# Attention transposes with a longer lag and a fourth buffer, and ScalarE as issuer of result stores, folds and four weight loads

## The chip, the cores and the metric

The kernel runs on one core of a Trainium2 chip. The metric is device microseconds of one execution, and less is better. The core has five instruction streams that matter here: TensorE (PE, with its weight loads shown as PEld), VectorE (DVE), ScalarE (ACT), GpSimd (POOL) and SyncE (SP). Each runs its own instructions in order and waits on semaphores for the others. A DMA transfer is started by an instruction on one of these engines, and the transfer itself runs on 16 DMA engines that all share.

## The reference

One layer of a hybrid decoder for a prompt of 2048 tokens and for 64 sample tokens (8 requests of 8 tokens) with a key/value cache of 2048 rows each. Cut to what matters:

```python
h = rms_norm(x, g_norm); proj = h @ w_in            # 1024 -> 3584
u, va, za, q, k, vb, zb = split(proj)               # q, k are RMS-normalised per head
a_out = rms_norm(u * (tril(w_s) @ rms_norm(va) + b_s)) * silu(za)   # mixer A, chunks of 128
for (w, r) in ((128, 1), (512, 4), (2048, 16)):     # mixer B, 8 heads of 64
    # query t attends to t - j*r, j = 0..w//r: regrouped by residue class,
    # blocks of 128 queries against their own and the previous block of keys
    s = q @ k.T * SCALE (masked); m = max(s); p = exp(s - m); den = sum(p)
    o_r = p @ v / den;  lse_r = m + log(den)
b_out = sum_r softmax(lse)_r * o_r                  # combine the three patterns
b = rms_norm(b_out) * silu(zb)
h = x + concat(a_out, b) @ w_out
y = h + sigmoid(h @ w_ple_gate) * rms_norm(p @ w_ple)
```

The outputs are y for prompt and samples, the window buffers k and v, the new k and v rows of the samples and the normalised va rows. Inputs and outputs are float32.

## The kernel before

All matrices are split into a high and a low float16 half, and a product is made of three float16 matmuls (two for the samples). The program has three stages in time.

The **projection stage** (0 to about 900 us) makes eight chunks of columns of `w_in` in the order A0, B0, B1, A1, B2, B3, A2, A3. A B chunk holds q, k, v and gate of one pair of heads, an A chunk holds u, va and za of one group. For a chunk, `wprep` loads eight blocks of weights (L351) into `wst` and converts them. `gemm` (L465 to L478) then runs 24 matmuls for each of 16 blocks of 128 tokens (L473). The 64 sample rows stand below them: their two halves come out in the upper and lower half of the partitions, `fold` (L480) copies the lower half (L483), moves it up by a DMA (L484) and adds. `b_evac`, `b_norm`, `b_trans`, `a_evac` and so on take the results out of PSUM; the evacuation of the gates of an A chunk is L617.

**Attention** runs inside this stage. There are 160 units, each one half of a group of four blocks, for 4 head pairs, 3 patterns and 4 groups. A unit has three steps:

- first (L733): `scores` makes the score matmuls (L823), masks them and takes the maximum on DVE (L829, L834), the exponentials on ACT (L838), the high half of the probabilities into tile `pc` on ACT (L841) and the low half on DVE (L842);
- mid (L761): one DMA transpose of `pc` into tile `pT`, issued by SP (L763);
- second (L765): `stage_c`, the products of `pT` with the values on PE (L869 to L871). After each second unit ACT moves the sums out of PSUM into `rec` (L875), and a DMA stores them to DRAM (L883) in `r1d`, `r2d` or `r3d`, one for each pattern. There are 96 of these stores.

The order of this work is set by `Pump` (L69 to L145). It keeps a modelled time `now`, which every two gemm matmuls move forward by their modelled length (L478). A unit's transpose becomes due `P_LAG` after its scores (L110), its product `T_LAG` after the transpose, and no more than `depth` units stand in each of the two waiting lists (L93, L102). The order written in this way is then placed on each engine by the scheduler of the framework, which goes by its own model. Tiles rotate: a tag with n buffers lets n tiles be alive, and the instruction that wants the next one waits for the last reader of the oldest. `pc` has 3 buffers, as `pT`.

When all groups of a head pair are stored, `comb_load` (L886) loads the three results (`rl`, L891) and the stored gate (`gzl`, L894), `combine` (L897) mixes and normalises them on DVE and ACT, its last two steps being L925 and L926, and stores the result to `catd` (L928).

In the **output stage** (about 960 us to the end) `p3_load` loads a block of `catd` (L1031), `halves_T` splits it (L995) and transposes it on SP (L996) into `Tc`, and `gemm2` makes the output and gate products (L1008). The weights of this stage are converted by `wprep3` (L965). The sample attention (`sample`, L1200) runs beside it on all engines. Among its tiles are K3 and qB (L1260, L1263, L1264) and V tiles, which share the tags of `pT`, `pc` and others. Between 900 and 960 us lies the transition: the last combine, its store, load, split and transpose must be through before the first output matmul.

Every DMA counts on one of eight completion semaphores, taken in turn over the whole program. An instruction that issues a DMA therefore also waits until the DMA eight places earlier has landed, whoever issued that one.

Of the kernel before, what the change touches and what calls it, by code (L numbers as in the profile page):

```python
# [11 lines left out]
F16 = mybir.dt.float16  # L12
F32 = mybir.dt.float32
# [8 lines left out]
P = 128  # L22
# [3 lines left out]
TS = 64  # L26
# [18 lines left out]
W_V3 = 3000.0  # L45

QK_LAG = 9000.0
P_LAG = 8500.0
T_LAG = 6500.0

PAIR_NS = 33700.0
# [96 lines left out]
def tile_hymba_gmlp_dilated_attn_step(  # L148
# [6 lines left out]
    nc = tc.nc  # L155
# [21 lines left out]
    cst = ctx.enter_context(tc.tile_pool(name="cst", bufs=1))  # L177
    sml = ctx.enter_context(tc.tile_pool(name="sml", bufs=4))
    drm = ctx.enter_context(tc.tile_pool(name="drm", bufs=1, space=DRAM))
    pump = Pump(3, P_LAG, T_LAG)  # L180
    uid = [0]

    def nm(s):
        uid[0] += 1
        return f"{s}_{uid[0]}"
# [78 lines left out]
    wk = ctx.enter_context(tc.tile_pool(name="wk", bufs=2))  # L264
# [76 lines left out]
    def wprep(kind, i, fast=False, room=None):  # L341
# [3 lines left out]
        for kp in range(4):  # L345
            t = room[:, kp] if room is not None else q4t([P, 2, 512], F32, "wst")
            for k2 in range(2):
                r0 = (2 * kp + k2) * P
                src = win[r0:r0 + P, c0:c0 + 512 * ns].rearrange("p (s c) -> p s c", c=512)[:, :, P * i:P * i + P]
                with after(ahead[0]) if room is not None else nullcontext():  # L350
                    nc.sync.dma_start(t[:, k2, :ncol].rearrange("p (s c) -> p s c", c=P), src)  # L351
                if room is not None:
                    yield 0.0
            st.append(t)
# [125 lines left out]
    def fold(g, n, tag, bufs=2):  # L480

        c = wk.tile([P, 512], F32, name=nm("fold"), tag=tag, bufs=bufs)
        nc.scalar.activation(c[TS:, :n], g[TS:, :n], AF.Copy)  # L483
        nc.sync.dma_start(c[:TS, :n], c[TS:, :n])  # L484

        def end():
            nc.vector.tensor_tensor(c[:TS, :n], c[:TS, :n], g[:TS, :n], op=ALU.add)
            return c
        return end
# [4 lines left out]
    def b_group(hp, jg, njt, m):  # L494
        ss = small(16, "bss", 2)
        if m < P:
            t = wk.tile([P, 512], F32, name=nm("sb"), tag="sb", bufs=1)
            cut = lambda a, b: t[:, a:b].unsqueeze(1)
            return dict(raw=cut(0, 256), vo=cut(256, 384), gz=cut(384, 512), ss=ss, n=njt, m=m, jg=jg, hp=hp)
        pump.run(lambda: len(v_open) < 3)  # L500
        v_open.append(0)
        raw = wk.tile([P, 4, 256], F32, name=nm("raw"), tag="raw", bufs=2)
        v16 = wk.tile([P, 4, 258], F16, name=nm("v16"), tag="v16", bufs=3)
        vo = wk.tile([P, 4, P], F32, name=nm("vo"), tag="tmpA", bufs=2)
        gz = wk.tile([P, 4, P], F32, name=nm("gz"), tag="gz", bufs=2)
        vv = v16.rearrange("p j (h c) -> p j h c", h=2)
        nc.vector.memset(vv[:, :, :, 64:65], 1.0)
        return dict(raw=raw, ss=ss, v16=v16, vv=vv, vo=vo, gz=gz, n=njt, m=m, jg=jg, hp=hp)
# [91 lines left out]
    def a_group(g, jg, njt, m):  # L600
        ss = small(4, "ass", 2)
        if m == P:
            ua = wk.tile([P, 4, 256], F32, name=nm("ua"), tag="raw", bufs=2)
            gz = wk.tile([P, 4, P], F32, name=nm("agz"), tag="gz", bufs=2)
        else:
            t = wk.tile([P, 512], F32, name=nm("sb"), tag="sb", bufs=1)
            ua, gz = t[:, 0:256].unsqueeze(1), t[:, 256:384].unsqueeze(1)
        u, va = ua[:, :, 0:128], ua[:, :, 128:256]
        return dict(ua=ua, u=u, va=va, gz=gz, ss=ss, n=njt, m=m, jg=jg, g=g)
# [200 lines left out]
    def scores(QH, QL, keys, r, sub):  # L810
# [26 lines left out]
            for h in range(2):  # L837
                nc.scalar.activation(sm4[:, s, h], sm4[:, s, h], AF.Exp, bias=r[:, sl + s, h, HD + 1:HD + 2])  # L838
        n = ns * 2 * kw
        pc = wk.tile([P, 1024], F16, name=nm("pc"), tag="pc", bufs=3)  # L840
        nc.scalar.activation(pc[:, :n], smv, AF.Copy)  # L841
        nc.vector.tensor_tensor(pc[:, n:2 * n], smv, pc[:, :n], op=ALU.subtract)  # L842
        return pc, n, 4 * ns * (kw * 0.416 + 8)
# [3 lines left out]
    def stage_c(hp, pat, grp, sub, r, pT):  # L847
# [26 lines left out]
        if sl + ns == 2:  # L874
            nc.scalar.activation(r[:, :, :, 0:65], po[:, :, :, 0:65], AF.Copy)  # L875
            rc = r.rearrange("p j h c -> p j (h c)")
            if pat == 3:
                dst = r3d[hp].rearrange("(p g j) c -> g p j c", g=4, j=4)[grp]
            elif pat == 2:
                dst = r2d[hp][grp * 512:(grp + 1) * 512].rearrange("(p j) c -> p j c", j=4)  # L880
            else:
                dst = r1d[hp][grp * 512:(grp + 1) * 512].rearrange("(j p) c -> p j c", p=P)
            nc.sync.dma_start(dst[:, s0:s0 + 2], rc)  # L883
        return ns * 6 * nb * 36.0

    def comb_load(hp, jg):  # L886
# [313 lines left out]
    def sample(hp):  # L1200
# [14 lines left out]
        seq = quads[0] + quads[1]  # L1215

        def load(name, src, tag="v"):
            t = wk.tile([P, 4, P], F32, name=nm(name), tag=tag, bufs=3)
            nc.sync.dma_start(t, src)
            return t  # L1220
        Ks = [loadK(seq[0]), loadK(seq[1])]
# [14 lines left out]
        for n in range(NB + 1):  # L1236
# [19 lines left out]
            for th in range(2 if n < NB else 0):  # L1256
                ts_ = slice(th * 4, th * 4 + 4)
                K3 = wk.tile([96, 4, P], F32, name=nm("K3"), tag="pT", bufs=3)
                nc.sync.dma_start(K3, ck[b, 0:1536, cs].rearrange("(i t) d -> i t d", t=16)[:, ts_])
                qB = wk.tile([96, 4, P], F32, name=nm("qB"), tag="pc", bufs=3)  # L1260
                src = qd[b * 8 + th * 4:b * 8 + th * 4 + 4, cs]
                nc.sync.dma_start(qB, src.unsqueeze(0).to_broadcast([96, 4, P]))
                nc.gpsimd.tensor_tensor(K3, K3, qB, op=ALU.mult)  # L1263
# [45 lines left out]
                           for b, tag in zip(quads[n % 2], tags[(n + 2) % 3])]  # L1309

        def V3load(src, tag):
            t = wk.tile([96, 4, P], F32, name=nm("V3"), tag=tag, bufs=3)
            nc.sync.dma_start(t, src)
            return t
        V3s = []
# [283 lines left out]
```

## Time and profile before

| | |
|---|---|
| device time, 3 runs | 1482.63, 1478.48, 1474.4 us; median 1478.48 us |
| profiled execution | 1471.11 us |
| its span (first to last instruction) | 1469.4 us |
| mean granted TensorE clock | 0.954 of full speed |
| busy: PE, DVE, ACT, POOL | 1296.9, 999.6, 821.8, 315.7 us |
| DMA | 271.32 MB, 185 GB/s in the mean |

Busy time leaves out what an engine spends on issuing DMAs, so the lines of SP in the views, named SPq, are issue times: how long the instruction held the queue. Start times count from the first instruction. In a view of waits, a row says which engine stood idle in front of an instruction of which line, and what released it. Numbers like L883 are lines of the program before. The changed program has one line more from L352 on, so L883 is there L884.

### The profile page before, as it was taken

The page shows a single profiled execution, that of the slowest core. Times are in us where ns is not written, and L with a number is a line of the kernel's source. Part 1 is how long each engine was busy: PE and PEld are TensorE (multiplying, and loading weights), DVE is VectorE, ACT ScalarE, POOL GpSimd, SP SyncE. Part 2 cuts the span into 40 slices and gives each one's busy share as a digit, 9 for nine tenths or more (in the row PEclk, how much of TensorE's full clock was granted, in tenths as well). Part 3 has the DMA queues.
Part 4 walks back from the last instruction along what each step waited for, and adds up shares of the span by engine and source line. Part 5 has one row for each costly group of instructions (what it writes and reads, how often), then busy time and mean ns, then how long its engine had stood idle before and what let it go on. Part 6 is the DMA issues. An engine that isn't in the chain of part 4 may idle for free.

```text
span 1469.4 us, 26262 instructions
## 1 busy us (share of the span) xinstructions
PE 1296.9 (88%) x8600; PEld 674.0 (46%) x8600; DVE 999.6 (68%) x3018; ACT 821.8 (56%) x2269; POOL 315.7 (21%) x279
## 2 busy tenths in 40 slices
PE   4899998998898897899788985569998998999998
PEld 2564454544564554455455653224443443444343
DVE  4675776777777698777778788885455456456364
ACT  5785778966679677687677884553222122123122
POOL 8221001102101111100120025311152143134001
PEclk9899999999999999999999998779999999999999
DMA  5954598799847989978996798976899799989542
GB/s 145 235 132 114 124 173 182 173 222 226 193 112 165 206 188 209 178 185 189 222 213 145 154 247 216 288 173 170 203 210 245 181 203 229 230 184 231 137 88 65
DMA packets 589592, 271.32 MB, mean 185 GB/s; under 512 B 323184, under 2 KB 571056, under 8 KB 589456
## 3 DMA queue, kind: packets, MB, share of 16 engines
q1 hardware_dynamic: 587472, 268.00, 80.7%
q0 software_dynamic: 1984, 1.66, 0.7%
q8 instruction: 67, 1.10, 0.3%
q14 instruction: 69, 0.57, 0.1%
HBM read 136.94 MB, written 55.08 MB: 131 GB/s over the span
## 4 chain that ended last, share of the span: by engine, by line
PE 44%; DMA 23%; DVE 14%; ACT 11%; issue 4%; SPq 3%; POOL 1%; DVEq 0%; ACTq 0%; POOLq 0%
PE psg L473 14%; PE psg L1008 11%; PE pss L1008 10%; DMA pT<-pc 6%; DMA rl<-r2d 2%; DVE sm L829 2%; ACT sm L838 2%; DMA K<-in_cache_k_dram 2%; DMA qB<-qd 2%; DMA wst<-in_w_in_dram 2%; PE pso L1343 2%; DVE pc L842 2%; PE pso L1248 2%; ACT kc L715 1%; DMA rl<-r3d 1%
## 5 line engine op out<-in xcount | busy, mean ns | idle before, releaser
L473 PE MATMUL psg<-wt,xT 128*128 128x512 f16 (+1 forms) x3072 | 640.6, 363 | 31.3 <-DVE agz L617 26.5
L473 PEld LDWEIGHTS <-xT 128*128 128x128 f16 x3072 | 301.7, 100 | 299.7 <-issue 44.3
L193 POOL TENSOR_TENSOR sm<-sm,mhalf 128x1 f32<-128x1 f32 (+5 forms) x115 | 145.6, 1271 | 790.4 <-DVE sm L532 324.6
L838 ACT ACTIVATE sm<-sm,rec 128x256 f32<-128x256 f32 (+1 forms) x384 | 151.7, 459 | 38.9 <-DVE rec L834 35.8
L829 DVE CUSTOM_DVE_ANT_0 sm<-pss,mask,psc 128x256 f32<-128x256 f32 (+1 forms) x384 | 145.1, 419 | 12.2 <-PE pss L823 8.5
L1008 PEld LDWEIGHTS <-Tc 128*128 128x128 f16 x800 | 76.8, 99 | 116.0 <-issue 28.5
L1263 POOL TENSOR_TENSOR K<-K,qB 96x512 f32<-96x512 f32 x64 | 94.1, 1475 | 161.2 <-DMA qB<-qd 62.3
L842 DVE TENSOR_TENSOR pc<-sm,pc 128x512 f16<-128x512 f32 (+1 forms) x160 | 104.2, 653 | 34.1 <-ACT pc L841 32.7
L1008 PEld LDWEIGHTS <-Th 128*128 128x128 f16 x800 | 76.7, 98 | 109.0 <-issue 15.3
L995 ACT ACTIVATE hl<-x,sm 128x1024 f16<-128x1024 f32 (+1 forms) x17 | 19.5, 1148 | 147.3 <-DVE sm L976 132.4
L869 PEld LDWEIGHTS <-pT 128*128 128x128 f16 x600 | 57.1, 98 | 96.1 <-DMA pT<-pc 90.5
L1008 PE MATMUL psg<-w,Th 128*128 128x512 f16 x400 | 95.8, 381 | 5.0 <-DMA Th<-hl 5.0
L841 ACT ACTIVATE pc<-sm 128x512 f16<-128x512 f32 (+1 forms) x160 | 96.0, 603 | 7.2 <-DMA pT<-pc 6.2
L1008 PE MATMUL psg<-w,Tc 128*128 128x512 f16 x400 | 97.0, 386 | 2.8 <-DMA Tc<-hl 2.8
L1264 DVE TENSOR_REDUCE blk<-K 96x8 f32<-96x512 f32 x64 | 43.4, 680 | 79.5 <-POOL K L1263 79.5
L1008 PE MATMUL pss<-w,Tc 128*128 128x512 f16 x400 | 96.0, 382 | 0.0
L1008 PE MATMUL pss<-w,Th 128*128 128x512 f16 x400 | 93.4, 379 | 0.0
L823 PEld LDWEIGHTS <-qk 128*128 128x128 f16 x960 | 74.2, 120 | 29.3 <-issue 5.9
L1100 POOL TENSOR_TENSOR tg<-tg,x 128x1024 f32<-128x1024 f32 (+1 forms) x16 | 37.6, 2348 | 153.9 <-DVE tg L1099 141.8
L869 PE MATMUL pso<-v,pT 128*128 128x65 f16 x248 | 32.2, 201 | 42.4 <-DMA pT<-pc 42.4
L869 PE MATMUL pso<-vt,pT 128*128 128x65 f16 x352 | 43.5, 195 | 28.9 <-DMA pT<-pc 28.8
L715 ACT ACTIVATE kc<-qk 128x512 f16<-128x512 f16 x72 | 58.9, 872 | 13.8 <-DMA qk<-qkd 8.5
(321 smaller groups left out, 2239.5 us busy)
## 6 DMA issues: line engine op xcount, KB each, us to landing
qB<-qd SPq DMA_DIRECT2D x64, 192.0 KB
K<-in_cache_k_dram SPq DMA_DIRECT2D x64, 192.0 KB
V<-in_cache_v_dram SPq DMA_DIRECT2D x64, 192.0 KB
vt<-vscr SPq DMA_DIRECT2D x32, 258.0 KB
K<-in_cache_k_dram SPq DMA_DIRECT2D x32, 256.0 KB
cat<-catd SPq DMA_DIRECT2D x16, 512.0 KB
x<-in_x_prompt_dram SPq DMA_DIRECT2D x16, 512.0 KB
V<-in_cache_v_dram SPq DMA_DIRECT2D x32, 256.0 KB
```

The costliest lines, as they stand in the source:

```text
L193: nc.gpsimd.tensor_tensor(y, src, mhalf[:p, :n], op=ALU.pow)
L473: last_mm[0] = nc.tensor.matmul(g[:, :ncol], lhsT=l, rhs=r, start=(n == 0), stop=(n == (23 if j < NT else 15)))
L715: nc.scalar.activation(t[:, h], src[:, h], AF.Copy)
L823: nc.tensor.matmul(pss[:, s, h, b * w:(b + 1) * w], lhsT=Q[:, h, qs], rhs=keys(h, k), start=(i == 0 and b == 0), stop=(i == 1 and b == n - 1))
L829: nc.vector.tensor_tensor_reduce(sm4[:, s, h], pss[:, s, h], mk, psc, -3.0e38, op0=ALU.add, op1=ALU.max, accum_out=mx[:, i:i + 1])
L838: nc.scalar.activation(sm4[:, s, h], sm4[:, s, h], AF.Exp, bias=r[:, sl + s, h, HD + 1:HD + 2])
L841: nc.scalar.activation(pc[:, :n], smv, AF.Copy)
L842: nc.vector.tensor_tensor(pc[:, n:2 * n], smv, pc[:, :n], op=ALU.subtract)
L869: nc.tensor.matmul(po[:, q, h, 0:65], lhsT=H, rhs=v[:, vs_, a:a + 65], start=(bi == 0), stop=False)
L1008: last_mm[0] = nc.tensor.matmul(gs[hf], lhsT=o[part][:, kt], rhs=w[:, kt % 2, half, :], start=(n[hf] == 0), stop=(n[hf] == (3 if m == P el ...
L1263: nc.gpsimd.tensor_tensor(K3, K3, qB, op=ALU.mult)
L1264: nc.vector.tensor_reduce(s3[:, b, :, ts_].rearrange("p h t -> p t h"), K3.rearrange("p t (h d) -> p t h d", d=HD), axis=AX.X, op=ALU.add)
```

## The change

It has four parts. `P_LAG` grows from 8500 to 11500 modelled ns, `Pump` may hold four units in each list, and the tag `pc` has four buffers (also for the sample tiles that use this tag). To make room for the fourth, the tile `sb` of folded sample rows, which had a buffer of its own, now uses the single buffer of `gzl`, which `comb_load` uses too. The 96 result stores and the 14 moves of folded rows are issued by ScalarE's queue (`nc.scalar`) in place of SyncE's. Of the eight weight loads of the first chunk (the call of `wprep` with `fast`), the four with odd index are issued by ScalarE too.

```diff
--- before.py
+++ after.py
@@ -45,7 +45,7 @@
 W_V3 = 3000.0
 
 QK_LAG = 9000.0
-P_LAG = 8500.0
+P_LAG = 11500.0
 T_LAG = 6500.0
 
 PAIR_NS = 33700.0
@@ -177,7 +177,7 @@
     cst = ctx.enter_context(tc.tile_pool(name="cst", bufs=1))
     sml = ctx.enter_context(tc.tile_pool(name="sml", bufs=4))
     drm = ctx.enter_context(tc.tile_pool(name="drm", bufs=1, space=DRAM))
-    pump = Pump(3, P_LAG, T_LAG)
+    pump = Pump(4, P_LAG, T_LAG)
     uid = [0]
 
     def nm(s):
@@ -348,7 +348,8 @@
                 r0 = (2 * kp + k2) * P
                 src = win[r0:r0 + P, c0:c0 + 512 * ns].rearrange("p (s c) -> p s c", c=512)[:, :, P * i:P * i + P]
                 with after(ahead[0]) if room is not None else nullcontext():
-                    nc.sync.dma_start(t[:, k2, :ncol].rearrange("p (s c) -> p s c", c=P), src)
+                    (nc.scalar if fast and k2 else nc.sync).dma_start(
+                        t[:, k2, :ncol].rearrange("p (s c) -> p s c", c=P), src)
                 if room is not None:
                     yield 0.0
             st.append(t)
@@ -481,7 +482,7 @@
 
         c = wk.tile([P, 512], F32, name=nm("fold"), tag=tag, bufs=bufs)
         nc.scalar.activation(c[TS:, :n], g[TS:, :n], AF.Copy)
-        nc.sync.dma_start(c[:TS, :n], c[TS:, :n])
+        nc.scalar.dma_start(c[:TS, :n], c[TS:, :n])
 
         def end():
             nc.vector.tensor_tensor(c[:TS, :n], c[:TS, :n], g[:TS, :n], op=ALU.add)
@@ -494,7 +495,7 @@
     def b_group(hp, jg, njt, m):
         ss = small(16, "bss", 2)
         if m < P:
-            t = wk.tile([P, 512], F32, name=nm("sb"), tag="sb", bufs=1)
+            t = wk.tile([P, 512], F32, name=nm("sb"), tag="gzl", bufs=1)
             cut = lambda a, b: t[:, a:b].unsqueeze(1)
             return dict(raw=cut(0, 256), vo=cut(256, 384), gz=cut(384, 512), ss=ss, n=njt, m=m, jg=jg, hp=hp)
         pump.run(lambda: len(v_open) < 3)
@@ -603,7 +604,7 @@
             ua = wk.tile([P, 4, 256], F32, name=nm("ua"), tag="raw", bufs=2)
             gz = wk.tile([P, 4, P], F32, name=nm("agz"), tag="gz", bufs=2)
         else:
-            t = wk.tile([P, 512], F32, name=nm("sb"), tag="sb", bufs=1)
+            t = wk.tile([P, 512], F32, name=nm("sb"), tag="gzl", bufs=1)
             ua, gz = t[:, 0:256].unsqueeze(1), t[:, 256:384].unsqueeze(1)
         u, va = ua[:, :, 0:128], ua[:, :, 128:256]
         return dict(ua=ua, u=u, va=va, gz=gz, ss=ss, n=njt, m=m, jg=jg, g=g)
@@ -837,7 +838,7 @@
             for h in range(2):
                 nc.scalar.activation(sm4[:, s, h], sm4[:, s, h], AF.Exp, bias=r[:, sl + s, h, HD + 1:HD + 2])
         n = ns * 2 * kw
-        pc = wk.tile([P, 1024], F16, name=nm("pc"), tag="pc", bufs=3)
+        pc = wk.tile([P, 1024], F16, name=nm("pc"), tag="pc", bufs=4)
         nc.scalar.activation(pc[:, :n], smv, AF.Copy)
         nc.vector.tensor_tensor(pc[:, n:2 * n], smv, pc[:, :n], op=ALU.subtract)
         return pc, n, 4 * ns * (kw * 0.416 + 8)
@@ -880,7 +881,7 @@
                 dst = r2d[hp][grp * 512:(grp + 1) * 512].rearrange("(p j) c -> p j c", j=4)
             else:
                 dst = r1d[hp][grp * 512:(grp + 1) * 512].rearrange("(j p) c -> p j c", p=P)
-            nc.sync.dma_start(dst[:, s0:s0 + 2], rc)
+            nc.scalar.dma_start(dst[:, s0:s0 + 2], rc)
         return ns * 6 * nb * 36.0
 
     def comb_load(hp, jg):
@@ -1215,7 +1216,7 @@
         seq = quads[0] + quads[1]
 
         def load(name, src, tag="v"):
-            t = wk.tile([P, 4, P], F32, name=nm(name), tag=tag, bufs=3)
+            t = wk.tile([P, 4, P], F32, name=nm(name), tag=tag, bufs=4 if tag == "pc" else 3)
             nc.sync.dma_start(t, src)
             return t
         Ks = [loadK(seq[0]), loadK(seq[1])]
@@ -1257,7 +1258,7 @@
                 ts_ = slice(th * 4, th * 4 + 4)
                 K3 = wk.tile([96, 4, P], F32, name=nm("K3"), tag="pT", bufs=3)
                 nc.sync.dma_start(K3, ck[b, 0:1536, cs].rearrange("(i t) d -> i t d", t=16)[:, ts_])
-                qB = wk.tile([96, 4, P], F32, name=nm("qB"), tag="pc", bufs=3)
+                qB = wk.tile([96, 4, P], F32, name=nm("qB"), tag="pc", bufs=4)
                 src = qd[b * 8 + th * 4:b * 8 + th * 4 + 4, cs]
                 nc.sync.dma_start(qB, src.unsqueeze(0).to_broadcast([96, 4, P]))
                 nc.gpsimd.tensor_tensor(K3, K3, qB, op=ALU.mult)
@@ -1309,7 +1310,7 @@
                            for b, tag in zip(quads[n % 2], tags[(n + 2) % 3])]
 
         def V3load(src, tag):
-            t = wk.tile([96, 4, P], F32, name=nm("V3"), tag=tag, bufs=3)
+            t = wk.tile([96, 4, P], F32, name=nm("V3"), tag=tag, bufs=4 if tag == "pc" else 3)
             nc.sync.dma_start(t, src)
             return t
         V3s = []
```

Three places show how the instructions stand. The first is SP's queue in an early stretch of attention, at the first groups of pattern 1 (`r1d`). Before:

```order
L883 DMA r1d_107<-rec_1640 128x2x132
L558 DMA zscr_103<-gz_1580 128x4x128
L763 DMA_TRANSPOSE pT_1948<-pc_1783 128x8x128
L351 DMA wst_2982<-in_w_in_dram 128x3x128 x2
L763 DMA_TRANSPOSE pT_1966<-pc_1803 128x4x128
L555 DMA out_dram<-ko_1860 128x4x128
L593 DMA_TRANSPOSE qk_256_1551<-qkc_1869 128x6x128
L593 DMA_TRANSPOSE qk_256_1551<-qkc_1875 128x6x128
L883 DMA r1d_107<-rec_1674 128x2x132
L763 DMA_TRANSPOSE pT_1983<-pc_1820 128x4x128
```

After:

```order
L764 DMA_TRANSPOSE pT_1853<-pc_1702 128x8x128
L559 DMA zscr_103<-gz_1580 128x4x128
L351 DMA wst_3005<-in_w_in_dram 128x3x128 x2
L764 DMA_TRANSPOSE pT_2035<-pc_1813 128x4x128
L556 DMA out_dram<-ko_1893 128x4x128
L892 DMA rl_4280<-r1d_107 128x4x132
L764 DMA_TRANSPOSE pT_2037<-pc_1830 128x4x128
L594 DMA_TRANSPOSE qk_256_1551<-qkc_1902 128x6x128
```

The two `r1d` stores are gone from between the transposes; a load `rl` of a combine has moved up.

The second place is ACT's queue around the evacuation `rec_1674`, whose store is the second of the two above. Before:

```order
L367 ACTIVATE junk_3082,sm_3079<-wst_2982,gno 128x384
L875 ACTIVATE rec_1674<-pso_1931 128x4x65
L838 ACTIVATE sm_1952<-sm_1952,rec_1950 128x128 x2
L841 ACTIVATE pc_1820<-sm_1809 128x256
L523 ACTIVATE vo_1896<-psg_2010,sm_1256 128x128
L525 ACTIVATE th_2130<-psg_2010,sm_1256 128x128
L841 ACTIVATE pc_1963<-sm_1952 128x256
L584 ACTIVATE qkc_1881<-raw_1577 128x2x64
```

After:

```order
L839 ACTIVATE sm_1819<-sm_1819,rec_1800 128x128 x2
L876 ACTIVATE rec_1674<-pso_1976 128x4x65
L524 ACTIVATE vo_1929<-psg_1932,sm_1256 128x128
L526 ACTIVATE th_2017<-psg_1932,sm_1256 128x128
L842 ACTIVATE pc_1830<-sm_1819 128x256
L884 DMA r1d_107<-rec_1674 128x2x132
L586 ACTIVATE qkc_1902<-raw_1577 128x256
L586 ACTIVATE qkc_1908<-raw_1577 128x256
```

The store stands on ACT, four rows behind the evacuation that feeds it and ahead of the conversion of the keys (`qkc`).

The third place is DVE at the transition, where the last steps of a combine (`gzl<-rl,gzl`, followed by its store) stand between conversions of output weights (`w<-w3st`) and sums of sample products (`blk<-K`). Before:

```order
L1264 TENSOR_REDUCE blk<-K_2441_13639 96x4x2
L925 TENSOR_TENSOR rl_12553<-rl_12553,sm_12678 128x8x64
L965 SCALAR_TENSOR_TENSOR w_2246_12769<-w3st_12312,sm_12701,w_2246_12769 128x512
L1264 TENSOR_REDUCE blk<-K_2446_13662 96x4x2
L965 SCALAR_TENSOR_TENSOR w_2246_12769<-w3st_12312,sm_12701,w_2246_12769 128x512
L965 SCALAR_TENSOR_TENSOR w_2247_12774<-w3st_12344,sm_12701,w_2247_12774 128x512
L1264 TENSOR_REDUCE blk<-K_2448_13668 96x4x2
L965 SCALAR_TENSOR_TENSOR w_2247_12774<-w3st_12344,sm_12701,w_2247_12774 128x512
L926 TENSOR_TENSOR gzl_12559<-rl_12553,gzl_12559 128x512
L965 SCALAR_TENSOR_TENSOR w_2250_12809<-w3st_12346,sm_12701,w_2250_12809 128x512
```

After:

```order
L618 SCALAR_TENSOR_TENSOR agz_12835<-th_12998,psg_12919 128x128
L1188 TENSOR_SCALAR blk<-blk 128x64
L1192 CAST sc_12868<-blk 128x16
L902 TENSOR_TENSOR sm_12933<-rl_12787,rl_12789 128x8
L924 TENSOR_SCALAR sm_12781<-sm_12781,sm_7116 128x8
L1194 TENSOR_SCALAR blk<-sc_12868,blk 128x16
L926 TENSOR_TENSOR rl_12613<-rl_12613,sm_12781 128x8x64
L966 SCALAR_TENSOR_TENSOR w_2227_12642<-w3st_12208,sm_12640,w_2227_12642 128x512
L927 TENSOR_TENSOR gzl_12619<-rl_12613,gzl_12619 128x512
L966 SCALAR_TENSOR_TENSOR w_2227_12642<-w3st_12208,sm_12640,w_2227_12642 128x512
```

Before, four weight conversions and two sample sums stand between the last two steps of the combine, and after it one conversion.

## Rows read from the trace of the kernel before

**Rows 1.** page, part 1: busy time, share of the span, instructions

```profile
PE 1296.9 (88%) x8600; PEld 674.0 (46%) x8600; DVE 999.6 (68%) x3018; ACT 821.8 (56%) x2269; POOL 315.7 (21%) x279
```

**Rows 2.** windows: stretch, length, busy by engine, clock, DMA share, GB/s

```profile
150.00:900.00 750.00, 664.21 (x5366) 385.69 (x5364) 573.31 (x2067) 564.69 (x1634) 112.72 (x84) 0.96 0.85 186
900.00:960.00 60.00, 31.40 (x131) 14.42 (x132) 53.98 (x109) 26.04 (x86) 26.43 (x19) 0.74 1.04 260
960.00:1470.00 510.00, 477.41 (x2366) 203.60 (x2364) 282.80 (x602) 133.03 (x292) 123.10 (x88) 0.97 0.80 182
```

**Rows 3.** waits of PE: us in all, times, longest us

```profile
PE pso L869 <- DMA pT<-pc: 71.2, 57, 3.4
```

**Rows 4.** waits of SP's queue: us in all, times, longest us

```profile
SPq L763 <- DVE pc L842: 59.5, 39, 6.0
SPq L883 <- ACT rec L875: 21.4, 21, 2.8
```

**Rows 5.** SP's instructions of L883, L763: count, ns min/median/max, first to last start

```profile
L883 SPq DMA_DIRECT2D r1d<-rec x32: 365/478/1178, 163.9 to 827.5; - x32
...
L883 SPq DMA_DIRECT2D r2d<-rec x32: 319/500/988, 182.5 to 881.6; - x32
...
L883 SPq DMA_DIRECT2D r3d<-rec x32: 319/429/2017, 272.3 to 869.8; - x32
...
L763 SPq DMA_TRANSPOSE pT<-pc x160: 1188/1248/4225, 153.5 to 876.1; - x160
```

**Rows 6.** windows of two full stretches of ACT

```profile
270.00:300.00 30.00, 28.18 (x236) 15.90 (x235) 25.67 (x102) 28.00 (x85) 2.90 (x1) 1.00 0.75 195
450.00:480.00 30.00, 26.64 (x235) 15.66 (x233) 21.23 (x99) 28.48 (x88) 3.58 (x5) 0.94 0.67 128
```

**Rows 7.** timeline of SP: start us, length us, instruction, count

```profile
691.36 0.64 SPq L883 DMA_DIRECT2D r2d<-rec  x1
692.10 1.40 SPq L763 DMA_TRANSPOSE pT<-pc  x1
693.54 3.95 SPq L597 DMA_TRANSPOSE qk<-qkd  x3
...
699.99 2.57 SPq L763 DMA_TRANSPOSE pT<-pc  x2
```

**Rows 8.** timeline of ACT: the evacuation that the store at 691.36 sends

```profile
682.79 0.37 ACT L875 ACTIVATE rec<-pso 128x260 f32<-128x260 f32 x1
```

**Rows 9.** timeline of PE near 702 us; in brackets idle before, releaser

```profile
702.50 0.20 PE L869 MATMUL pso<-v,pT 128*128 128x65 f16 x1 [1.01 <-DMA pT<-pc]
```

**Rows 10.** timeline of SP, transition

```profile
869.78 0.53 SPq L883 DMA_DIRECT2D r3d<-rec  x1
...
908.99 1.10 SPq L928 DMA_DIRECT2D catd<-gzl  x1
...
918.07 0.46 SPq L1031 DMA_DIRECT2D cat<-catd  x1
...
931.04 2.99 SPq L996 DMA_TRANSPOSE Tc<-hl  x1
```

**Rows 11.** timeline of DVE, transition

```profile
885.02 0.68 DVE L912 TENSOR_TENSOR rl<-rl,rl 128x520 f32<-128x520 f32 x1
...
908.28 0.68 DVE L926 TENSOR_TENSOR gzl<-rl,gzl 128x512 f32<-128x512 f32 x1
```

**Rows 12.** timeline of PE, transition

```profile
883.02 12.84 PE L473 MATMUL psg<-wt,xT 128*128 128x384 f16 x78
...
912.13 5.70 PE L473 MATMUL psg<-wt,xT 128*128 128x384 f16 x24 [14.97 <-DVE agz L617]
...
939.18 2.75 PE L1008 MATMUL pss<-w,Tc 128*128 128x512 f16 x12
```

**Rows 13.** window of the first weight loads

```profile
3.00:16.00 13.00, 0.00 (x0) 0.00 (x0) 2.31 (x9) 3.87 (x10) 8.63 (x18) 1.00 0.99 260
```

## The prediction

> **What bounds the kernel now.** I read the busy times first, then windows by stage, then waits, then timelines. PE is busy 88% of the span [rows 1]; DVE and ACT have slack over the whole, so the question is where PE stands idle. By stage [rows 2], PE is idle 750 − 664 = 86 us in the stretch with attention, 29 us in the 60 us of the transition and 33 us in the 510 us of the output stage. The reader is to see that the middle row is no average of the others: its PE is half empty at a granted clock of 0.74, against 0.96 and 0.97.
>
> In the attention stretch one wait stands out: PE's products wait for the transposed probabilities 57 times, 71.2 us in all and 3.4 at most [rows 3]. Why is `pT` late? SP waits for `pc` before only 39 of its 160 transposes [rows 4, 5]; in front of the other 121 it had nothing to wait for and came late itself. So most of the 71.2 us is SP's queue and the short lag, not the making of `pc`. A picture of it: from 691.36 us on SP issues a store, one transpose of `pc`, three of keys (3.95 us) with more work on keys behind them, and from 699.99 on two more of `pc`, with hardly a pause [rows 7]; the product at 702.50 waits 1.01 us for the last of them [rows 9].
>
> **The change part by part.** All terms are set against the profiled execution, 1471.1 us, of which 1469.4 are span. That is 7.4 us under the median of the runs shown (1478.48), so I add the sum to the median in the end. What a measurement can tell from no change is about 0.5%, also 7.4 us.
>
> *Stores leave SP.* 96 stores at medians of 0.478, 0.500 and 0.429 us, on average 0.47 [rows 5], make 45 us of SP's time. SP also no longer stands in wait for `rec` in front of them, 21.4 us in 21 times [rows 4], which held up whatever was behind. What reaches PE is less: only what was ahead of a transpose that PE waited for. I count one store fewer ahead of each of the 57 waits: 57 × 0.47 = 27 us. The bounds are 0 (another instruction takes the place) and 71.2 (the lag and the fourth buffer end the wait altogether). The lag helps less than 8500 to 11500 suggests, since the scheduler places the rows again; where the rows show it, the distance from scores to product grows little, by three or four gemm matmuls. I take −27, the value of the nearest rows.
>
> *Stores come onto ACT.* The trace has no DMA issued by ACT; the nearest rows are SP's, from 0.32 to 2.0 us each [rows 5], so 96 × 0.32 = 31 us up to 192 us on ACT. Over the stretch ACT has 750 − 565 = 185 us idle [rows 2], and at the median the 45 us fit. Not everywhere: in 270 to 300 us and in 450 to 480 us ACT is busy 28.0 and 28.5 of 30 [rows 6]. Eight stores in such a stretch are 3.4 us against 2.0 and 1.5 us of room, so up to 2 us run over; with four such stretches 8 us. A store also waits, in order, for `rec` (free on ACT itself, which writes it) and for the DMA eight places earlier. What is behind it on ACT is the exponentials, the next `pc` and the conversions of keys. I add 3 us for stores that are held. Cost +11; bounds 0 and 38 (worked out under the third rival). The 14 folds go the same way, and their evacuation is on ACT too: 0, at most +1.
>
> A rule speaks against this part. The Trainium skill (DMA: Bandwidth & Descriptors, "Issuing engines are not separate DMA queues") says that DMAs started by different engines end up on the same 16 DMA engines, and that a second issuer saves only the sequencer's time to start them, usually little beside the transfer. By that rule at most the 45 us of issue can be won. The trace has SP's queue without pauses just there, so the saved issue is worth something here, and my −27 is under that ceiling.
>
> *The end of attention moves.* By the order of the rows, before 246 gemm matmuls stand behind the last product of pattern 3, and after 172. Attention thus ends 74 matmuls later; at 12.84 / 78 = 0.165 us for one (78 of them from 883.02 us on take 12.84 us [rows 12]) that is +12 us. With −27 + 11 = −16 it ends 4 us earlier on the clock.
>
> *The transition.* From the last store of pattern 3 (869.78 us) to the first output matmul (939.18) the chain takes 69.4 us [rows 10, 12], and most of it is not transfer: between the sum of the three patterns (ends 885.7) and the combine's last step (908.28) lie 22.6 us in which DVE works through conversions and sample sums [rows 11]; the store follows at 908.99, the load of `cat` at 918.07, the transposes at 931.04 [rows 10]. PE fills this only in part: at 912.13 it has stood 14.97 us waiting for a gate's evacuation by the same DVE [rows 12]. In the new order one conversion stands between the last two steps of the combine where four and two sums stood, and fewer rows further up, so I let that piece shrink to about 8 us: −14. SP has 6 rows fewer of K3 and qB loads ahead of the store to `catd`, and the evacuations stand closer: −6 more. Together −20; bounds 0 (the piece moves to another row of the chain) and −29, all of PE's idle time in the window. Set against attention's end, 4 us earlier, PE starts the output stage 24 us earlier. The output stage has the same order from its middle on and 33 us of idle time, and I leave it unchanged.
>
> *Smaller edits.* `sb` and `gzl` share one buffer, so an evacuation of sample rows waits for the store of a combine, and at four places a `gzl` load waits on SP for the stores of the sample rows. By the order these stand 2 to 4 rows apart, so the price is a landing each; 0 to 8 us, I take +2. The first weights: DMA engines are busy 0.99 from 3 to 16 us [rows 13], so a second issuer finds no free engine: 0, within 1.5 us either way. Four buffers for qB and V in the samples: 0, at best −5.
>
> Sum: −27 + 11 + 12 − 20 + 2 = −22. By the profiled execution's time 1449 us, by the median 1456.
>
> **Rivals.**
> *The lag does its full work.* With four units and buffers in flight each transpose has a unit more of time, the longest wait of 3.4 us is covered, and of 71.2 us only the waits behind bursts are left, say 15. Then −56 + 11 + 12 − 20 + 2 = −51, which gives 1428. For it: no wait is long [rows 3]. Against: the distance in the rows grows little, and SP's queue, not the buffer, is what was late.
>
> *The transition gives it back.* Attention's end moves by +12, and the chain behind it keeps its 69.4 us with fewer gemm matmuls to fill it. Then −16 + 12 + 2 = −2: 1476, no change. For it: the chain crosses five engines, and the piece on DVE can be replaced by another, as DVE is busy 54 of 60 us there [rows 2]. Against: fewer rows stand ahead in the new order.
>
> *ScalarE is held by its stores.* SP took some stores late: a `rec` ended at 683.16 us and its store went out at 691.36 [rows 7, 8], 8 us behind; there are two more like it. If what held them is the DMA eight places earlier rather than SP's backlog, ACT stands in these places, and with it the exponentials. Three such places are 24 us, the full stretches with none of their slack used 4 × 3.4 = 14: 38 us in place of 11. The chain, fed by the same ACT, then gives only half, −10: −27 + 38 + 12 − 10 + 2 = +15, that is 1493. With the chain at −20 the change turns into a loss from 33 us held on ACT, with −10 from 23. For it: ACT is in order and full in places. Against: most late stores stood behind transposes on SP and not behind a landing.
>
> The Trainium skill (TensorE: Matmul & The Clock Gate, the specification table) gives ScalarE a strictly first-in-first-out queue, so a held store would hold the exponentials; no run here shows a DMA on ACT's queue yet. By that rule the third rival's time is the consequence wherever a store is held at all.
>
> **How the numbers follow.** My forecast 0.42: 1456, its own range 1440 to 1471 with ACT's cost between 0 and 20 and the chain between −10 and −29. The first rival 0.18 (1428), the second 0.20 (1476), the third 0.20 (1493). Faster by over 0.5% (below 1471) is the forecast and the first rival: 0.60. Within 0.5% is the second, 0.20; slower is the third, 0.20. The range for 8 in 10 goes from 1425, the middle of the first rival, to 1492, where half of the third lies beyond.
>
> **What would show it.** Right: PE's waits for `pT` at about 45 us; ACT's queue with 110 issues near 0.5 us and no wait of more than 1 us for a landing; the first output matmul near 915 us in the span, 24 earlier. The first rival shows in waits under 20 us, the second in a first output matmul near 937 us. The third shows as waits of ACT in front of L883's stores and of PE's products or DVE's `pc` for ACT. I am wrong at the root if the waits for `pT` stay at 70 us although SP has lost 45 us of issue.

## The result, and the profile after

The changed kernel takes 1491.72 us in the median of 7 runs (1486.97 to 1497.57), the kernel before 1474.63 (1470.25 to 1482.63). The ratio is 1.0114, with a 95% interval of 1.009 to 1.0137: 17 us slower, where 22 us faster was forecast. That it lies just inside the range, whose upper end was 1492, is owed to the third rival's share in it. The profiled execution took 1487.63 us, its span 1485.6, 16.2 us more than before. Of the 104 runs of the experiments below, one (in the first of them) took 4617.94 us and is left out of its ratio and its median.

The windows of the same stretches as in [rows 2] come first:

```profile
150.00:900.00 750.00, 672.35 (x5461) 391.68 (x5458) 580.17 (x2099) 567.07 (x1647) 114.08 (x85) 0.97 0.87 189
900.00:960.00 60.00, 25.41 (x88) 9.99 (x89) 52.06 (x102) 28.04 (x80) 22.59 (x14) 0.66 1.05 247
960.00:1470.00 510.00, 469.46 (x2299) 199.17 (x2298) 277.35 (x586) 124.73 (x281) 118.70 (x88) 0.97 0.80 179
```

In the attention stretch PE is idle 78 us instead of 86: 8 us are won there. The transition loses more, 34.6 us idle instead of 28.6 in its first 60 us, and the stretch behind it 41 us instead of 33. Cut at 1020 us, PE's idle time of the whole span divides like this (span less busy time; 172.5 us before, 189.2 after):

| PE idle, us | 0 to 150 | 150 to 900 | 900 to 1020 | 1020 to end |
|---|---|---|---|---|
| before | 26.2 | 85.8 | 39.9 | 20.6 |
| after | 30.4 | 77.6 | 57.5 | 23.7 |

So the question is what happens between 900 and 1020 us. PE's waits in the changed kernel (us in all, times, longest):

```profile
PE pso L870 <- DMA pT<-pc: 62.6, 53, 5.3
PE psg L1009 <- DMA Tc<-hl: 23.5, 2, 16.8
...
PE pst L655 <- issue: 15.3, 1, 15.3
PE psg L1009 <- DVE agz L618: 13.9, 1, 13.9
```

The first row answers to [rows 3]. The second and the fourth lie mostly in front of the first output matmul (16.75 and 13.88 us); there the kernel before waits too, for the gates of an A chunk:

```profile
PE psg L473 <- DVE agz L617: 26.5, 3, 15.0
```

The third has no counterpart before: one matmul, L655, before which PE stands 15.3 us, nearly all of the 17.6 us more of idle time between 900 and 1020 us. It belongs to the spatial mixing of the 64 sample rows of the last A chunk, and reads the tile `sb`. PE's timeline there:

```profile
930.61 1.03 PE L1009 MATMUL psg<-w,Tc 128*128 128x512 f16 x2 [16.75 <-DMA Tc<-hl]
...
1000.68 0.65 PE L655 MATMUL pst<-sb,bd 64*64 64x128 f32 x2 [15.31 <-issue]
1001.51 5.75 PE L1009 MATMUL psg<-w,Tc 128*128 128x512 f16 x20 [0.18 <-DVE e L1082]
1007.19 0.27 PE L1225 MATMUL pst<-ident,blk 64*128 64x64 f32 x1
```

The view calls the releaser "issue", that is, none that it sees. ACT's timeline gives it:

```profile
990.78 0.63 ACT L916 ACTIVATE rl<-rl 128x512 f32<-128x512 f32 x1 [3.33 <-DVE rl L913]
998.25 0.42 ACT L614 ACTIVATE sb<-fold 64x256 f32<-64x256 f32 x1 [6.84 <-DMA catd<-gzl]
```

ACT writes `sb` at 998.25, and waited for the transfer `catd<-gzl`, which has nothing to do with the sample rows except that `gzl` is now the same buffer. SP's timeline has the four combines' stores of the last head pair:

```profile
894.37 0.37 SPq L929 DMA_DIRECT2D catd<-gzl  x1
...
902.74 1.07 SPq L1032 DMA_DIRECT2D cat<-catd  x1
...
924.35 2.21 SPq L997 DMA_TRANSPOSE Tc<-hl  x1
...
939.49 0.37 SPq L929 DMA_DIRECT2D catd<-gzl  x1
...
981.92 0.37 SPq L929 DMA_DIRECT2D catd<-gzl  x1
...
995.79 0.37 SPq L929 DMA_DIRECT2D catd<-gzl  x1
```

The sample rows come behind the fourth, 2.5 us after it is issued. Their folded sum was there from 930.95 on:

```profile
884.27 0.68 DVE L913 TENSOR_TENSOR rl<-rl,rl 128x520 f32<-128x520 f32 x1
...
893.66 0.68 DVE L927 TENSOR_TENSOR gzl<-rl,gzl 128x512 f32<-128x512 f32 x1
...
930.40 0.55 DVE L488 TENSOR_TENSOR fold<-fold,psg 64x384 f32<-64x384 f32 x1 [0.72 <-DMA fold<-fold]
```

Data that is ready at 930.95 waits 67 us for a buffer. In the kernel before, ACT and PE handle the same rows thus, the first with no wait at all:

```profile
951.36 0.40 ACT L613 ACTIVATE sb<-fold 64x256 f32<-64x256 f32 x1
```

```profile
965.30 0.43 PE L654 MATMUL pst<-sb,bd 64*64 64x128 f32 x2
...
969.66 0.27 PE L1224 MATMUL pst<-ident,blk 64*128 64x64 f32 x1
```

The theory I took from this: the shared buffer is the loss. The rivals were that the transition is bound by the combine and its loads, so that removing this wait only uncovers others, and that ScalarE is held by its stores.

### The profile page after: what moved, and what is told of

It reads as the page before. It is cut to its first block, busy times and chain, and to the rows that moved or that the text cites. A ratio compares the mean times of both kernels' runs of the same rounds, so it can differ in the third digit from the quotient of the medians.

```text
span 1485.6 us, 26176 instructions
## 1 busy us (share of the span) xinstructions
PE 1296.4 (87%) x8600; PEld 672.3 (45%) x8600; DVE 1002.9 (68%) x3018; ACT 819.7 (55%) x2269; POOL 311.8 (21%) x279
## 3 DMA queue, kind: packets, MB, share of 16 engines
q0 software_dynamic: 1984, 1.66, 0.7%
## 4 chain that ended last, share of the span: by engine, by line
PE 28%; DMA 18%; DVE 7%; ACT 3%; SPq 2%; issue 2%; POOL 1%; POOLq 0%; ACTq 0%; DVEq 0%
PE psg L1009 8%; PE pss L1009 8%; PE psg L474 6%; DMA pT<-pc 4%; DMA qB<-qd 3%; DMA K<-in_cache_k_dram 2%; PE pso L1344 2%; PE pso L1249 2%; DMA V<-in_cache_v_dram 1%; POOL K L1264 1%; DMA rl<-r3d 1%; DMA Tc<-hl 1%; PE pss L824 1%; PE pst L1244 1%; DMA rl<-r2d 1%
## 5 line engine op out<-in xcount | busy, mean ns | idle before, releaser
L474 PEld LDWEIGHTS <-xT 128*128 128x128 f16 x3072 | 298.6, 100 | 273.4 <-issue 26.1
L839 ACT ACTIVATE sm<-sm,rec 128x256 f32<-128x256 f32 (+1 forms) x384 | 151.5, 460 | 28.6 <-DVE rec L835 27.3
L1009 PEld LDWEIGHTS <-Tc 128*128 128x128 f16 x800 | 77.2, 100 | 141.1 <-issue 34.5
L1009 PE MATMUL psg<-w,Tc 128*128 128x512 f16 x400 | 101.5, 397 | 23.6 <-DMA Tc<-hl 23.5
L1101 POOL TENSOR_TENSOR tg<-tg,x 128x1024 f32<-128x1024 f32 (+1 forms) x16 | 37.6, 2348 | 156.6 <-DVE tg L1100 96.6
L1254 ACT ACTIVATE KT<-pst 128x512 f32<-128x512 f32 x32 | 19.0, 595 | 92.8 <-PE pst L1244 83.1
```

Of the source, the lines that this page charges most:

```text
L474: last_mm[0] = nc.tensor.matmul(g[:, :ncol], lhsT=l, rhs=r, start=(n == 0), stop=(n == (23 if j < NT else 15)))
L1009: last_mm[0] = nc.tensor.matmul(gs[hf], lhsT=o[part][:, kt], rhs=w[:, kt % 2, half, :], start=(n[hf] == 0), stop=(n[hf] == (3 if m == P el ...
```

## The experiments

Ratios are to the kernel before, with 95% intervals.

**The last sample rows apart.** Only the rows of the last A chunk leave `gzl`.

```diff
-t = wk.tile([P, 512], F32, name=nm("sb"), tag="gzl", bufs=1)          # a_group
+t = wk.tile([P, 512], F32, name=nm("sb"), tag="pc" if g == 3 else "gzl", bufs=4 if g == 3 else 1)
```

> The changed kernel, but the folded sample rows of the last A chunk take a buffer of the tag pc and not the one of gzl. Theory: most of the loss is that these rows wait for the last combine's store, with PE standing 15.3 us in front of the sample matmul L655; without the wait the time falls by 11 to 15 us, to 1.002 (1.000 to 1.004) of before, and PE's wait in front of L655 is under 3 us. Rival (the transition is bound by the combine and its loads, the wait only hides others): the waits for Tc and Th grow instead, and the ratio stays at 1.009 to 1.012. Rival (ScalarE held by its stores in attention): also unchanged, 1.011.

0.9947 (0.9927 to 0.9966), 1467.6 us in the median of five runs: the loss is gone and more than the 15 us in front of L655, 1.67% or 24 us. ACT writes the rows at 923.70 and PE reads them without a wait:

```profile
923.70 0.42 ACT L614 ACTIVATE sb<-fold 64x256 f32<-64x256 f32 x1 [0.34 <-DVE fold L488]
```

```profile
937.69 0.43 PE L655 MATMUL pst<-sb,bd 64*64 64x128 f32 x2
```

PE then waits 18.1 us for a transpose `Th`, where it waited 6.2 in the changed kernel, so the rival had a grain of truth, but the time fell nonetheless.

**The kernel before, rows shared.** The opposite edit, with nothing else of the change.

```diff
-t = wk.tile([P, 512], F32, name=nm("sb"), tag="sb", bufs=1)     # b_group and a_group
+t = wk.tile([P, 512], F32, name=nm("sb"), tag="gzl", bufs=1)
```

> The kernel before with one edit: the folded sample rows use the buffer of gzl. Theory: PE stands some 15 us in front of the last sample matmul as in the changed kernel, and the time is 11 to 16 us over before, ratio 1.009 (1.007 to 1.011). Rival (the transition is bound elsewhere): within 4 us, ratio 1.000 to 1.003. Rival (ScalarE held by its stores): 1.000, since no store is on ScalarE here.

1.0168 (1.0145 to 1.0191), 25 us lost, more than I expected. PE's last sample matmul:

```profile
1007.47 0.65 PE L654 MATMUL pst<-sb,bd 64*64 64x128 f32 x2 [8.37 <-issue]
```

PE's wait there is 8.4 us and not the 15 that I expected, although the loss is larger, so the standing in front of this matmul is not the whole price. The sharing alone makes the kernel before slower than the changed one.

**First weights back on SyncE**, in the changed kernel and, with the last rows apart, in the first experiment's; and **the split alone** in the kernel before.

```diff
-(nc.scalar if fast and k2 else nc.sync).dma_start(
+nc.sync.dma_start(
```

> The changed kernel with all eight first weight loads back on SyncE. Theory: the start loses 4 us by the split (PE's idle time up to 120 us is 30.4 in the changed kernel and 26.2 before), because the token loads come forward and share the DMA engines with the weights; without it the ratio falls from 1.011 to 1.0085. Rival (the start's 4 us come from elsewhere, such as chance in GpSimd's loads): unchanged, 1.011.

> The changed kernel with the last folded sample rows in a buffer of pc and all first weight loads on SyncE. In the profiles PE's idle time in the first 120 us is 26.2 to 30.7 for the same program, so theory now: the split is worth nothing, ratio as with the rows apart, 0.995 (0.992 to 0.998). Rival (the split costs 3 to 4 us at the start): 0.992.

> The kernel before with only the four odd weight loads of the first chunk issued by ScalarE. Theory: DMA engines are busy there already, 1.000 (0.998 to 1.002). Rival (token loads come forward and the first matmul is later): 1.002 to 1.003, first gemm matmul 2 us later than 21.65.

1.0091 (1.0067 to 1.0114), 0.9946 (0.9924 to 0.9968) and 0.9998 (0.998 to 1.0016). The 4 us that the start seemed to lose is mostly the spread between profiles: PE's idle time up to 120 us is 26.2, 30.7, 28.7, 27.3, 29.8, 28.3 and 29.2 us in seven profiles with all loads on SyncE, and 28.5 to 31.0 in seven with the split (the means differ by 1.6 us, and the times of the split alone show no loss). Against the changed kernel the first ratio fell by 0.0023, within the intervals.

**Stores alone** and **lag alone**, in the kernel before.

```diff
-nc.sync.dma_start(c[:TS, :n], c[TS:, :n])
+nc.scalar.dma_start(c[:TS, :n], c[TS:, :n])
-nc.sync.dma_start(dst[:, s0:s0 + 2], rc)
+nc.scalar.dma_start(dst[:, s0:s0 + 2], rc)
```

> The kernel before with only the 96 result stores and the 14 folds moved to ScalarE; lag, depth and buffers as before. Theory: the attention stretch gains its 8 us by the stores leaving SyncE (waits for the transposed probabilities 71 to about 60 us), and nothing is lost elsewhere: ratio 0.995 (0.992 to 0.998). Rival (the gain of the stretch is the lag's, and the stores cost ScalarE as much as they free on SyncE): 1.000 (0.998 to 1.002). Rival (ScalarE held by its stores): 1.005 to 1.010, with ScalarE's waits in front of the stores over 15 us.

```diff
-P_LAG = 8500.0
+P_LAG = 11500.0
-pump = Pump(3, P_LAG, T_LAG)
+pump = Pump(4, P_LAG, T_LAG)
```

> The kernel before with only the lag of 11500 and depth 4; three buffers of pc, stores on SyncE, folded rows in their own buffer. Theory (the gain that is left when the sample rows stand apart, 0.5%, comes from the lag and the buffers, since the stores alone gave 0.9993): 0.996 (0.993 to 0.999). Rival (the lag needs the fourth buffer, since pc is given back only after its transpose): 1.000 to 1.003. Rival (neither matters alone, it is the order at the transition): anything from 0.995 to 1.010, set by PE's waits between 890 and 1010 us and not by those for the transposed probabilities.

0.9993 (0.9975 to 1.0011) and 0.9989 (0.997 to 1.0007): alone, each is worth nothing that can be told. With the stores alone, SP waits longer for `pc` than in [rows 4], while PE still waits 65.8 us for `pT`:

```profile
SPq L763 <- DVE pc L842: 89.5, 50, 6.6
```

Of the time that SP won, 30 us went into longer waits for `pc` (89.5 us instead of 59.5).

**Own rows, three buffers of pc.** All of the change but the fourth buffer and the sharing that pays for it.

```diff
-name=nm("sb"), tag="gzl", bufs=1        # both groups
+name=nm("sb"), tag="sb", bufs=1
-tag="pc", bufs=4                        # and 3 for the sample tiles
+tag="pc", bufs=3
```

> The changed kernel, but with the folded sample rows in their own buffer as before and three buffers of pc; lag, depth and ScalarE's DMAs as changed. Theory (the shared buffer is the loss, the fourth buffer is worth little): 0.996 (0.993 to 1.000). Rival (the fourth buffer is what lets the lag work): 1.000 to 1.005, with waits for the transposed probabilities back at 71 us or above. Rival (the loss is in the other parts): 1.010.

0.9878 (0.9848 to 0.9908), 1458.47 us: faster than both kernels, and better than I expected. PE's waits for `pT` and its first sample matmul there:

```profile
PE pso L870 <- DMA pT<-pc: 53.9, 45, 4.0
```

```profile
941.90 0.40 PE L655 MATMUL pst<-sb,bd 64*64 64x128 f32 x2 [2.15 <-issue]
```

**The last rows shared again in that kernel, and in the kernel before.**

```diff
-name=nm("sb"), tag="sb", bufs=1         # a_group
+name=nm("sb"), tag="gzl" if g == 3 else "sb", bufs=1
```

> The kernel with own sample rows and three buffers of pc (0.988), but the rows of the last A chunk in the buffer of gzl. Theory: the wait comes back, 1.007 (1.002 to 1.012), 20 us or more above the kernel without it. Rival (part of the 0.988 is a lucky order that any edit destroys): the time rises, but the last sample matmul does not come later than 970 us.

> The kernel before with only the folded rows of the last A chunk in the buffer of gzl, the other seven in their own. Theory (the last rows alone are the loss, because only they stand behind all four combines of the last head pair): 1.016 (1.011 to 1.020), near the 1.017 with all eight shared, and PE's last sample matmul (L654) at about 1008 us as there, against 965.5. Rival (the sharing costs over the whole attention stretch): half of it or less, 1.000 to 1.008.

1.0044 (1.0023 to 1.0064), which is 0.0166 above the kernel with own rows, and 1.0115 (1.0082 to 1.0148). In the first, ACT's wait is back, and PE's with it:

```profile
986.86 0.42 ACT L614 ACTIVATE sb<-fold 64x256 f32<-64x256 f32 x1 [6.84 <-DMA catd<-gzl]
```

```profile
989.27 0.66 PE L655 MATMUL pst<-sb,bd 64*64 64x128 f32 x2 [13.73 <-issue]
```

Attention ends there as in the kernel with own rows (last product at 867.7 and 865.3 us; 880.4 before), so all of the difference arises behind it. Between 900 and 1020 us PE is idle 50 us instead of 34. The windows of 900 to 1020 us, own rows first:

```profile
900.00:1020.00 120.00, 86.14 (x374) 37.10 (x374) 90.50 (x214) 49.80 (x125) 27.45 (x19) 0.85 0.85 213
```

```profile
900.00:1020.00 120.00, 70.04 (x288) 29.90 (x289) 85.15 (x195) 44.54 (x105) 25.47 (x20) 0.77 0.78 194
```

Over the whole span the same matmuls keep PE busy 1295.3 us instead of 1283.6. The 16 us more of idle time and 12 of busy time, less 5.5 us of idle time elsewhere, are the 22 us between the two spans (1472.4 and 1450.1).

The 12 us of busy time are no standing still. The granted clock between 900 and 1020 us is 0.77 instead of 0.85, a mixture of the levels 1.2 and 2.4 GHz, but over the whole span PE is busy 65.8 us at the lower level instead of 63.7 (counted from the trace), which makes about 1 us, as the lower level is half of the upper. Some 8.5 us lie in the output stage, in the 128 products of the sample values (L1344, with 32 columns of weights and 512 of values). The window of these products alone from 900 to 1500 us (length, PE's busy time, clock, DMA share, GB/s), own rows first:

```profile
900.00:1500.00 600.00, 28.57 (x128) 0.96 0.76 175
```

```profile
900.00:1500.00 600.00, 37.61 (x128) 0.94 0.76 175
```

They stand among the output matmuls in runs, and a run of two takes as long as one of eight (rows of the kernel with the last rows shared):

```profile
1260.80 1.07 PE L1344 MATMUL pso<-V,blk 96*32 96x512 f32 x8
...
1266.66 1.05 PE L1344 MATMUL pso<-V,blk 96*32 96x512 f32 x2
```

With own rows there are 27 such runs, with the last rows shared 35. The order on PE is the scheduler's, so the edit costs in two ways: it makes PE wait at the transition, and it comes with an order that splits these products. Why the order comes out so is not shown.

In the kernel before, the last rows alone cost 1.15% (0.82 to 1.48), 17 us; the idle time in front of the matmul is 6.85 us there:

```profile
998.97 0.65 PE L654 MATMUL pst<-sb,bd 64*64 64x128 f32 x2 [6.85 <-issue]
```

Of the 14.8 us between the profiled spans there (1484.2 and 1469.4), 6.2 are idle time and 8.6 busy time, and the sample products again go from 26 runs to 35 (27.4 to 37.6 us in the same window).

**Three buffers of pc, rows shared**, and **all rows in a buffer of pc**.

```diff
-tag="pc", bufs=4                        # first kernel, from the changed one
+tag="pc", bufs=3
```

```diff
-name=nm("sb"), tag="gzl", bufs=1        # second kernel, from the changed one
+name=nm("sb"), tag="pc", bufs=4
```

> The changed kernel with three buffers of pc, the folded sample rows still in the buffer of gzl. Theory (the shared buffer is the loss, and the fourth buffer of pc is worth nothing): as the changed kernel, 1.011 (1.006 to 1.017). Rival (the fourth buffer itself costs, and that is why the kernel with own rows and three buffers is 0.988): under 1.000.

> The changed kernel with all folded sample rows in a buffer of pc (four buffers in all), none in that of gzl. Theory (what separates 0.995 with the last rows apart from 0.988 with all rows in their own buffer is the seven earlier sharings with gzl): 0.988 (0.984 to 0.992). Rival (it is the fourth buffer, or the order that the scheduler makes of it): 0.995 as with the last rows apart.

1.0092 (1.0064 to 1.012) and 0.9929 (0.9905 to 0.9954). In the first the fourth buffer of `pc` is worth nothing that can be told while the rows share (1.0114 with it). The second lies between its theory and its rival and does not decide: lending one of four buffers to the rows is not the same as a buffer of their own.

## Why the prediction was wrong

**The step that failed is the price of the shared buffer**, "0 to 8 us, I take +2". Measured with three buffers of `pc` in both kernels, all eight sharings cost 2.1% (1.0092 against 0.9878), 32 us. I priced a landing at each place where a `gzl` load stands behind the sample rows' stores, and left the other direction at the same: sample rows behind a combine's store. There are two sizes of that. Inside the projections a combine is soon over: the seven earlier sharings cost 0.5% (1.0092 against 1.0044, and 1.0168 against 1.0115 in the kernel before; the intervals of each pair just touch). At the end the last rows stand in turn behind four combines, the last of which is stored at 995.79, and they were ready 65 us earlier. That costs 1.15% in the kernel before, 1.66% with own rows (1.0044 against 0.9878) and 1.67% in the changed one (1.0114 against 0.9947, where the last rows lie in a buffer of `pc`). About half of it is idle time of PE, as the theory had it; much of the rest is the order of the sample products, which neither the prediction nor the theory had.

**The rest of the sum was near, but not by its terms.** Without the sharing's +2, my sum was −24 us; all of the change without sharing and fourth buffer is 0.9878, −18 us (−22 to −14). That is luck in part. The gains in the sum are all time that PE stands idle, but of the 19.3 us between the profiled spans only 6.0 are idle time (172.5 to 166.5); 13.3 are busy time, and PE is busy 63.7 us at the lower clock level instead of 89.8 (counted from the traces; half of the difference is 13 us). The mean granted clock of all runs is 0.961 against 0.956 in the kernel before.

I gave −16 of the sum to the stores, yet the stores alone give nothing (0.9993), nor does the lag alone (0.9989). What the two give together they do not give singly. That SP waits 89.5 us for `pc` once its stores are gone speaks for the lag being needed to use the freed queue, but it does not show it: the order of the sample products moves too, with 33 and 30 runs in place of 26 (35.5 and 31.6 us in the window instead of 27.4, and 28.6 with both), which by itself is more than half of the 15 us that the two lack singly. Whether the two need each other stays open.

**ScalarE's cost of +11 was too high.** The 96 stores on ACT (ns min/median/max):

```profile
L884 ACTq DMA_DIRECT2D r1d<-rec x32: 372/377/437, 166.7 to 825.2; - x32
L884 ACTq DMA_DIRECT2D r2d<-rec x32: 326/338/398, 184.9 to 888.4; - x32
L884 ACTq DMA_DIRECT2D r3d<-rec x32: 326/330/665, 279.0 to 864.2; - x32
```

They are shorter than on SP [rows 5]. ACT's row of waits leaves out its own issues, but the trace has the times: ACT stands idle for over 0.05 us before only three of the 96, 0.6 us at most. So the third rival, which gave the right time (1493), gave it for a wrong reason: ACT's stores go out 0.03 us after `rec` in the median and 2.4 us at most. The strictly first-in-first-out queue of the Trainium skill (TensorE: Matmul & The Clock Gate, the specification table) was not contradicted; no store kept ACT idle for longer than those 0.6 us. It is at the `sb` row that ACT, and PE behind it, stood.

**The waits for the transposes** fell from 71.2 to 62.6 us, not to 45, and to 53.9 with own rows. One store per wait was too much: of −27 us came 8.6, and 17 with own rows. The reading behind it was wrong as well. From [rows 4] I took that SP had nothing to wait for in front of 121 transposes, but the same view has more waits of them under other names, such as:

```profile
SPq L763 <- DVE sm L829: 22.5, 11, 4.2
...
SPq L763 <- PE pso L871: 21.2, 20, 1.6
```

By the times in the trace, SP's queue stood empty for over 0.15 us before 62 of the 160, 93 us in all, so SP was late by its own backlog less often than I had it.

**The attention's end.** The order's count was right (74 gemm matmuls less stay behind the last product of pattern 3). That product started at 861.9 us, against 857.3, where I had it 4 us earlier; but its store, freed of SP's queue, went out at 864.16 instead of 869.78. The last product of all started at 882.8 us, against 880.4.

**The chain at the transition** gave −3 and not −20: from the last store of pattern 3 (864.16 us) to the first output matmul (930.61) it takes 66.4 us instead of 69.4. The piece on DVE shrank as predicted, from 22.6 to 8.7 us (L913's end at 884.95 to 893.66). But the load of `cat` to its transpose, 13.0 us before [rows 10], now takes 21.6, and the way to L913 5 us more. Of the bounds I gave, "0 (the piece moves to another row of the chain)" was the nearer one. The first output matmul on `Tc` still came 8.6 us earlier, and the stop at L655 took more than that back.

**The start** was right: the split is worth nothing, 0.9998. The rule of the Trainium skill (DMA: Bandwidth & Descriptors, "Issuing engines are not separate DMA queues") held in that place: the DMA engines were busy already [rows 13].

The order itself had shown the failed step: it puts the last L655 behind 162 output matmuls, where L654 stood behind 91 before. In all of the kernels that share the last rows it is 162, in the others at most 91. The prediction left that out.

## What to carry to other kernels

When a tile moves into another tile's single buffer, follow both users to their last instance and ask which in-order engine stands behind the one that comes second. The price can be far more than a landing: here a tile waited 67 us, and 17 to 24 us reached the end, partly as idle time of PE and partly by the order that came with it. Where a scheduler places the instructions, compare the orders before putting a difference down to a wait. And try the parts without the buffer that they were thought to need: here the fourth buffer was not worth its room.

## What the runs showed of the hardware that was not expected

Two things. A DMA that ACT issued cost ACT little, since most of the issue ran beside ACT's own work. In the changed kernel the 96 stores took 34.5 us of issue, of which, counted store by store, 24.4 lie under a running ACT instruction. One of them, with the rows around it:

```profile
855.80 0.64 ACT L950 ACTIVATE junk<-w3st 128x512 bf16<-128x512 f32 x1
855.95 0.33 ACTq L884 DMA_DIRECT2D r3d<-rec  x1
856.32 0.21 ACT L950 ACTIVATION_READ_ACCUMULATOR junk<-w3st 128x1 f32 x1
```

The store starts at 855.95, inside the instruction that began at 855.80, and the next one comes at its usual distance.

The other is the time of the sample products L1343 and L1344. From the start of a run to the next matmul it took 0.98 us in the median for two of them and 1.00 us for eight, so that eight more runs of the same 128 matmuls cost 8.5 us.
